# Attention score products of two heads side by side: queries and keys kept as pairs of heads on 128 rows

## The chip, the cores and the metric

The kernel runs on one core of a Trainium2 chip. A core has five engines with instruction queues of their own: TensorE (PE) multiplies matrices into PSUM, VectorE (DVE) and ScalarE (ACT) work element by element and read PSUM, GpSimd (POOL) works from SBUF, and SyncE (SP) issues DMAs. The metric is the device time of one execution in microseconds, the median of the runs.

## The reference

Two post-norm layers over 512 tokens of width 1024, in f32. Heads have 64 dimensions, so two heads fill the 128 partitions.

```
layer 0: proj = x @ w_in_swa                       # 12 query heads, 3 key/value heads, 4 memory queries
         q, k = partial_rope(q), partial_rope(k)   # the first 16 of 64 dimensions rotate
         self = softmax over {two chunks back and own chunk of 64 keys, sink} . v
         cross = softmax(qc . km * scale) . vm     # 4 heads, 256 memory tokens
         x = layer_norm(a*x + [self, cross] @ w_out); x = layer_norm(a*x + swiglu(x))
layer 1: proj = x @ w_in_fox                       # 12 query, key and value heads, 4 memory queries, 12 forget logits
         cum = cumsum(log_sigmoid(f_logit + b))
         self = softmax(q . k * scale + cum[query] - cum[key], causal) . v
         cross as above, out projection and norm as above
         x = layer_norm(a*x + moe(x))              # top 2 of 8 SwiGLU experts
```

## The kernel before

Every f32 operand is split into two f16 parts, high (f32 times a scale, rounded by an ACT copy, `high`) and low (what is left, by a DVE subtraction, `low`), and a product is three: high x high, high x low, low x high (`mm3`, L236). Weights arrive as chunks of 1 MB on SP's queue into three raw buffers; `Weights.tick` (L163) lets ACT write the high part of a piece (L149) and DVE the low one (L158). Seven split chunks are held (`NHL`). The order of all instructions is written out by hand (`manual_schedule`): each engine works through its own list in order.

The stages are: prologue and memory projections (0 to 54 us), sliding-window attention with memory heads (54 to 205), dense SwiGLU (205 to 580), forgetting layer (580 to 762 for its attention), out projection and routing (to 820), experts (to the end).

Attention goes in items. An item is one block of 128 queries against the keys that it sees: four memory heads (256 keys), four query heads of one key head (128 or 256 keys), or a pair of forgetting heads (128 to 512 keys). There are 8, 12 and 24 of them. `Att.step` (L589) runs items in a pipeline of four steps: scores (S, L488), maximum and exponentials (M), normalisation (N), transposes of the weights P (T, L545), low parts (L), output product (O, L562). ORDS and ORDX (L69) say in which order a step issues these, with a fill (F: a projection needed later) and weight ticks (W). In layer 0 the order is W F S O T M L N, in layer 1 w F S T M N L O. So in PE's list a fill comes ahead of the scores.

A fill of the forgetting layer is `qk_fill` (L1068): 24 products of 256 columns into a PSUM bank, then the evacuation of two heads' keys or queries. There are four such banks (L225), shared with the transposes and outputs.

How queries and keys are kept now:

- Queries have the high part of a head on 64 rows and its low part on the other 64 (`q_evac`, L398: two ACT copies, two DVE subtractions for a pair of heads). Keys have the high part of each head twice, on both halves (`k_evac`, L410: four ACT copies), and the low part once, two heads on 128 rows (two DVE subtractions). So one product over 128 rows gives (q high + q low) x k high (L497).
- The third product, q high x k low, works on 64 rows; for memory and forgetting heads those of two heads stand next to each other on different halves of the array (L506). Sliding-window keys are twice on 128 rows in both parts, and the product with the low part runs over 128 rows (L501).
- Masks and bias are added by products (L499): sliding window, an identity times a mask over all keys of the item; forgetting, a selector of 96 rows (three bf16 parts of the running sum for 12 heads) times the sums, and an identity times the causal mask.
- Rotary queries are turned by four transposes per token block, one per head, onto 64 rows (L823 to L826).

Of the kernel before, what the change touches and what calls it, by code (L numbers as in the profile page):

```python
# [209 lines left out]
def trunk_kernel(ctx, tc, x, mem, positions, w_in_swa, attn_sinks, w_in_fox, b_forget, w_mem_kv, w_out,  # L210
# [113 lines left out]
    identb = base.tile([128, 128], BF, name="identb")  # L324
    nc.vector.tensor_scalar(identb, jp, 0.0, None, op0=OP.is_equal)
# [72 lines left out]
    def q_evac(Q, i, n, src, sc, cols):  # L398

        todo = []  # L400
        for half in range(2):
            a, b = halves(half)
            idx = slice(i + half, i + half + 2 * n - 1, 2) if n > 1 else i + half
            todo.append((Q[a, idx, cols], Q[b, idx, cols], src(half)))
        for h, _, s in todo:
            high(h, s, sc)
        for h, l, s in todo:
            low(l, s, sc, h)

    def k_evac(KH, KL, heads, src, sc, cols):  # L410

        for half in range(2):
            for r in halves(half):
                high(KH[r, heads(half), cols], src(half), sc)
        for half in range(2):
            a = halves(half)[0]
            low(KL[a], src(half), sc, KH[a, heads(half), cols])

# [69 lines left out]
    def att_scores(it):  # L488
        nh, nk = it["nh"], it["nk"]
        b2 = bank2()  # L490
        it["S"] = b2.rearrange("p a n -> p (a n)").rearrange("p (h n) -> p h n", h=nh)[:, :, :nk]
        bank_of = lambda i: i * 2 // nh
        for i in range(nh):
            h = it["order"][i]
            o = it["S"][:, i, :]
            first = i == 0 or bank_of(i) != bank_of(i - 1)
# [3 lines left out]
            if it["rows"] is None:  # L500
                nc.tensor.matmul(o, it["q"](h), it["kl"](h), start=False, stop=True, skip_group_check=True)  # L501
        if it["rows"] is not None:
            for i in sorted(range(nh), key=lambda i: i % (nh // 2)):
                h = it["order"][i]
                a = it["rows"](h)
                nc.tensor.matmul(it["S"][:, i, :], it["q"](h)[a], it["kl"](h)[a], start=False, stop=True,  # L506
                                 skip_group_check=True)
# [108 lines left out]
    def mem_items(Qm, KM, VM, sp, blk0):  # L616
        for b in range(NT):
            bq = slice(b * 128, b * 128 + 128)
            yield dict(nh=MH, nk=ML, order=(0, 2, 1, 3), rows=lambda h: halves(h % 2)[0], pool=sp, sink=None, b=b,
                       blk=blk0, add=lambda h: [], q=lambda h, bq=bq: Qm[h // 2][:, h % 2, bq],  # L620
                       kh=lambda h: KM[0][:, h, :], kl=lambda h: KM[1][:, h // 2, :],
                       v=lambda h, kb: [v[:, kb, h * HD:h * HD + HD] for v in VM])

    def mem_kv(u, memT, KM, VM):
        def kpair(p):
# [3 lines left out]
            for k in range(KD):  # L629
                mm3(b, wh[:, k, c], wl[:, k, c], memT[0][:, k, :], memT[1][:, k, :], k == 0, k == KD - 1)  # L630
            k_evac(KM[0], KM[1][:, p, :], lambda hf: 2 * p + hf, lambda hf: b[64 * hf:64 * hf + 64, :], DS * SQ,
                   slice(0, ML))
# [14 lines left out]
    def qc_proj(wh, wl, c0, Qm):  # L647
        for p in range(MH // 2):
# [4 lines left out]
            q_evac(Qm[p], 0, 1, lambda hf: b[64 * hf:64 * hf + 64, :], DS * SQ, slice(0, S))  # L653
# [47 lines left out]
    def mem_tiles(pool):  # L701
        return ((pool.tile([128, MH, ML], FH, name="KMh"), pool.tile([128, MH // 2, ML], FH, name="KMl")),
# [15 lines left out]
    nc.gpsimd.dma_start(sinks, bass.AP(tensor=attn_sinks.tensor, offset=attn_sinks.offset, ap=[[0, 128], [1, NH]]))  # L718
    smask = sp.tile([128, 256], BF, name="smask")
    nc.vector.memset(smask, 0.0)  # L720
    nc.vector.memset(smask[0:64, 192:256], NEG)
    nc.vector.memset(smask[64:128, 0:64], NEG)
# [15 lines left out]
    KL = sp.tile([128, 3, S], FH, name="KL")  # L738
    V = (sp.tile([128, NT, 192], FH, name="Vh"), sp.tile([128, NT, 192], FH, name="Vl"))
    Qm = sp.tile([128, 4, S], FH, name="Q4", bufs=3)  # L740
    Qm = [Qm[:, 0:2], Qm[:, 2:4]]
# [16 lines left out]
    nc.vector.tensor_copy(posf, pos)  # L758
    for j in range(8):
        nc.vector.tensor_scalar(ang[:, :, j], posf, INV_FREQ[j], None, op0=OP.mult)  # L760
# [52 lines left out]
    def rope_evac(g, qk, t):  # L813
# [8 lines left out]
        else:  # L822
            for k in range(4):  # L823
                nc.tensor.transpose(b[:64, k, :], qk[:, k, :], identf)
            high(Qg[g][0:64, :, c], b[0:64])
            low(Qg[g][64:128, :, c], b[0:64], 1.0, Qg[g][0:64, :, c])  # L826

    def swa_items(g):
        for b in range(NT):
# [4 lines left out]
            yield dict(nh=4, nk=nk, order=range(4), rows=None, pool=sp, b=b, blk=2 * g,  # L834
                       sink=sinks[:, 4 * g:4 * g + 4], add=lambda h, nk=nk: [(0, nk, identb, smask[:, 256 - nk:])],
                       q=lambda h, bq=bq: Qg[g][:, h, bq],
                       kh=lambda h, kc=kc: KH[:, g, kc], kl=lambda h, kc=kc: KL[:, g, kc],
# [6 lines left out]
    def swa_fill(which):  # L844
# [6 lines left out]
        if t == 0 and g is not None:  # L851
            Qg[g] = sp.tile([128, 4, S], FH, name="Q4", bufs=3)
# [1012 lines left out]
```

## Time and profile before

| what | value |
|---|---|
| median of 3 runs | 1661.68 us (1661.27 to 1664.03) |
| profiled execution | 1663.01 us; its span 1661.2 us |
| TensorE busy, weight loads busy | 1596.2 us, 1281.7 us |
| VectorE, ScalarE, GpSimd busy | 1229.1 us, 975.3 us, 266.0 us |
| mean granted clock of TensorE | 0.989 of full speed |
| HBM | 355.08 MB read, 12.39 MB written |

The span runs from the first to the last instruction. The busy time of TensorE counts a product from its start to its modelled end, and products overlap, so what one costs in a stream is the distance to the next one's start. "Idle before" is the time for which an engine stood still ahead of an instruction, and the releaser is what ended that. DVE and ACT work through their lists in order, so an evacuation can stand behind work that has nothing to do with it.

### The profile page before, as it was taken

To read this page: it belongs to the slowest core of one execution; us is meant where nothing else is said; L and a number is where in the kernel's file an instruction comes from. 1 tells how busy PE (TensorE), PEld (TensorE's weight loads), DVE (VectorE), ACT (ScalarE), POOL (GpSimd) and SP (SyncE) were. 2 spreads that over 40 slices of the span, in tenths; PEclk is the share of its full clock that TensorE was granted. 3 is DMA by queue.
4 is the path that set the end of the run, shared out by engine and by line. 5 is a ranking of instruction groups with operands and counts; after the bars stand their busy time and mean duration, and the time that the engine had idled before them with its cause. 6 is when DMAs were issued, how large, how long until landed. Compare 5 with 4: busy or idle time off the path is not lost.

```text
span 1661.2 us, 42749 instructions
## 1 busy us (share of the span) xinstructions
PE 1596.2 (96%) x18452; PEld 1281.7 (77%) x18452; DVE 1229.1 (74%) x1826; ACT 975.3 (59%) x1499; POOL 266.0 (16%) x264
## 2 busy tenths in 40 slices
PE   7998999999999999999799999999999999999996
PEld 6785664444444747765699999999999999999994
DVE  6798643333534568786899698996979979699997
ACT  6776243333211457664477677776877778665773
POOL 0443100000200000003130140201303031130251
PEclk9999999999999999999899999999999999999998
DMA  7511033332631142111699899999999999999993
GB/s 266 178 52 52 3 127 125 102 102 90 213 120 54 52 129 75 52 52 39 224 353 335 301 387 387 371 349 304 389 362 371 364 315 376 336 289 370 349 369 126
DMA packets 180531, 370.13 MB, mean 223 GB/s; under 512 B 6573, under 2 KB 49581, under 8 KB 180336
## 3 DMA queue, kind: packets, MB, share of 16 engines
q1 hardware_dynamic: 173264, 343.48, 57.9%
q0 software_dynamic: 4768, 15.47, 4.0%
q10 hardware_dynamic: 2304, 8.39, 1.4%
q8 instruction: 146, 2.39, 0.6%
q14 instruction: 49, 0.40, 0.1%
HBM read 355.08 MB, written 12.39 MB: 221 GB/s over the span
## 4 chain that ended last, share of the span: by engine, by line
PE 43%; issue 3%; POOL 2%; ACT 1%; DVE 1%; DMA 1%; POOLq 0%; ACTq 0%; DVEq 0%
PE bk L1401 9%; PE bk L1403 9%; PE bk L1402 9%; PE bk L1432 4%; PE bk L1430 4%; PE bk L1431 4%; ACT wh L149 1%; POOL act L1419 1%; PE bk L239 1%; PE bk L237 1%; PE bk L238 1%; DVE wl L158 1%; POOL expert_sums L1334 1%; PE bk L1451 1%; PE bk L1342 1%
## 5 line engine op out<-in xcount | busy, mean ns | idle before, releaser
L158 DVE SCALAR_TENSOR_TENSOR wl<-raw,wh 128x1048 f16<-128x1048 f32 (+3 forms) x654 | 794.4, 1264 | 105.0 <-ACT wh L149 104.7
L149 ACT ACTIVATE wh<-raw 128x1048 f16<-128x1048 f32 (+3 forms) x654 | 640.9, 1041 | 100.2 <-PE bk L239 40.4
L1401 PE MATMUL bk<-xa,wh 128*128 128x160 f16 (+3 forms) x1280 | 261.2, 232 | 5.6 <-DMA lng<-in_ln_ffn_g_dram 5.6
L1402 PE MATMUL bk<-xa,wh 128*128 128x160 f16 (+3 forms) x1280 | 261.1, 232 | 0.0
L1403 PE MATMUL bk<-xa,wl 128*128 128x160 f16 (+3 forms) x1280 | 261.1, 232 | 0.0
L1401 PEld LDWEIGHTS <-wh 128*128 128x128 f16 x2560 | 250.9, 98 | 6.4 <-issue 5.7
L1402 PEld LDWEIGHTS <-wh 128*128 128x128 f16 x2560 | 250.9, 98 | 2.7 <-issue 2.4
L1403 PEld LDWEIGHTS <-wl 128*128 128x128 f16 x2560 | 251.0, 98 | 0.0
L1432 PE MATMUL bk<-act,wl 128*128 128x160 f16 (+6 forms) x1232 | 235.3, 227 | 1.2 <-DVE wl L158 1.2
L1430 PE MATMUL bk<-act,wh 128*128 128x160 f16 (+6 forms) x1232 | 235.3, 227 | 0.0
L1431 PE MATMUL bk<-act,wh 128*128 128x160 f16 (+6 forms) x1232 | 235.2, 227 | 0.0
L1401 PE MATMUL bk<-xe,wh 128*128 128x128 f16 (+2 forms) x1280 | 223.2, 221 | 2.2 <-DVE sa L1417 1.4
L1403 PE MATMUL bk<-xe,wl 128*128 128x128 f16 (+2 forms) x1280 | 223.1, 221 | 0.0
L1402 PE MATMUL bk<-xe,wh 128*128 128x128 f16 (+2 forms) x1280 | 223.1, 221 | 0.0
L237 PE MATMUL bk<-xTh,wh 128*128 128x512 f16 (+2 forms) x656 | 206.5, 325 | 7.7 <-DVE KLx L234 6.2
L239 PE MATMUL bk<-xTh,wl 128*128 128x512 f16 (+2 forms) x656 | 206.1, 324 | 2.8 <-DVE wl L158 2.8
L238 PE MATMUL bk<-xTl,wh 128*128 128x512 f16 (+2 forms) x656 | 206.2, 324 | 0.5 <-DVE xTl L234 0.5
L1419 POOL TENSOR_TENSOR act<-sa,act 128x512 f16<-128x512 f32 (+6 forms) x40 | 106.9, 2673 | 282.4 <-ACT act L231 282.4
L237 PEld LDWEIGHTS <-wh 128*128 128x128 f16 x944 | 93.1, 99 | 57.7 <-DVE KLx L234 7.2
L239 PEld LDWEIGHTS <-wl 128*128 128x128 f16 x944 | 93.2, 99 | 52.1 <-DVE wl L158 4.9
L238 PEld LDWEIGHTS <-wh 128*128 128x128 f16 x944 | 93.3, 99 | 47.5 <-issue 1.6
L1432 PEld LDWEIGHTS <-wl 128*128 128x128 f16 x1232 | 120.5, 98 | 1.6 <-DVE wl L158 1.6
(350 smaller groups left out, 2756.1 us busy)
## 6 DMA issues: line engine op xcount, KB each, us to landing
raw<-in_w_exp_in_dram SPq DMA_DIRECT2D x176, 1024.0 KB, 8.5
raw<-in_w_exp_out_dram SPq DMA_DIRECT2D x85, 1024.0 KB, 8.9
raw<-in_w_ffn_in_dram SPq DMA_DIRECT2D x22, 1024.0 KB, 5.4
raw<-in_w_out_dram SPq DMA_DIRECT2D x8, 1024.0 KB, 5.1
raw<-in_w_ffn_out_dram SPq DMA_DIRECT2D x8, 1024.0 KB, 5.6
raw<-in_w_in_fox_dram SPq DMA_DIRECT2D x8, 1024.0 KB, 5.3
raw<-in_w_mem_kv_dram SPq DMA_DIRECT2D x4, 1024.0 KB, 6.9
raw<-in_w_in_swa_dram SPq DMA_DIRECT2D x4, 896.0 KB, 8.9
```

Source lines behind the costliest of these rows:

```text
L149: self.nc.scalar.activation(h[:, p:e], t[:, p:e], AF.Copy, scale=SW)
L158: self.nc.vector.scalar_tensor_tensor(l, src, SW, h, op0=OP.mult, op1=OP.subtract)
L237: nc.tensor.matmul(o, lh, rh, start=first, stop=False, **kw)
L238: nc.tensor.matmul(o, lh, rl, start=False, stop=False, **kw)
L239: nc.tensor.matmul(o, ll, rh, start=False, stop=last, **kw)
L1401: nc.tensor.matmul(o, wh[:, k, c], xe[0][:, k, :C], start=first, stop=False, skip_group_check=True)
L1402: nc.tensor.matmul(o, wh[:, k, c], xe[1][:, k, :C], start=False, stop=False, skip_group_check=True)
L1403: nc.tensor.matmul(o, wl[:, k, c], xe[0][:, k, :C], start=False, stop=k == KD - 1, skip_group_check=True)
L1419: lambda: nc.gpsimd.tensor_sub(act[1][:, j, :C], sa[:, :, :C], act[0][:, j, :C])]
L1430: nc.tensor.matmul(o, wh[:, k, c], act[0][:, kk, :C], start=first, stop=False, skip_group_check=True)
L1431: nc.tensor.matmul(o, wh[:, k, c], act[1][:, kk, :C], start=False, stop=False, skip_group_check=True)
L1432: nc.tensor.matmul(o, wl[:, k, c], act[0][:, kk, :C], start=False, stop=kk == KF - 1, skip_group_check=True)
```

## The change

Queries and keys of two heads are kept as one tile of high parts and one of low parts, both on 128 rows (head A on rows 0 to 63, head B on 64 to 127). An evacuation is then one ACT copy and one DVE subtraction. All three score products of a head run on its 64 rows, and so do bias and mask. They are issued in turn for two heads of a pair, whose results go to two different PSUM banks:

```diff
-            nc.tensor.matmul(o, it["q"](h), it["kh"](h), start=first, stop=False, skip_group_check=True)
-            for lo, n, a, bb in it["add"](h):
-                nc.tensor.matmul(o[:, lo:lo + n], a, bb, start=False, stop=False, skip_group_check=True)
...
+        for pr in range(nh // 2):
+            both = [(half, it["S"][:, pr + half * nh // 2, :], it["parts"](2 * pr + half)) for half in range(2)]
+            n = len(both[0][2])
+            for j in range(n):
+                for half, o, parts in both:
+                    lo, m, r, a, c = parts[j]
+                    r = halves(r)[0]
+                    nc.tensor.matmul(o[:, lo:lo + m], a[r], c[r], start=pr == 0 and j == 0, stop=j == n - 1,
+                                     skip_group_check=True)
+    def products(h, nk, Q, K):
+        return [(0, nk, h % 2, Q[i], K[k]) for i, k in ((0, 0), (1, 0), (0, 1))]
```

Evacuations, in `mem_kv`, `qc_proj` and `qk_fill`:

```diff
-            if which:
-                k_evac(QK[p][1], QK[p][2][:, r], lambda hf: hf, src, DS * SQ, r)
-            else:
-                q_evac(QK[p][0], 0, 1, src, DS * SQ, r)
+            o = QK[p][which]
+            high(o[:, 0, r], b, DS * SQ)
+            low(o[:, 1, r], b, DS * SQ, o[:, 0, r])
```

Rotary queries (two transposes of two heads each), sliding-window mask (only the edges of 64 keys that need one) and forgetting bias and mask (64 rows):

```diff
-            for k in range(4):
-                nc.tensor.transpose(b[:64, k, :], qk[:, k, :], identf)
-            high(Qg[g][0:64, :, c], b[0:64])
-            low(Qg[g][64:128, :, c], b[0:64], 1.0, Qg[g][0:64, :, c])
+            for k in range(2):
+                nc.tensor.transpose(b[:, k, :], qk[:, 2 * k:2 * k + 2, :].rearrange("p i d -> p (i d)"), identf)
+            high(Qg[g][0][:, :, c], b[:, :2, :])
+            low(Qg[g][1][:, :, c], b[:, :2, :], 1.0, Qg[g][0][:, :, c])
...
+                edges = [(nk - 64, 64, h % 2, half_id[:, 0], smask)] + [(0, 64, h % 2, half_id[:, 1], smask)] * (nk > 128)
+                return products(h, nk, [q[:, h // 2, bq] for q in Qg[g]], [k[:, g, kc] for k in KHL]) + edges
...
+                return products(h, nk, [Q[:, i, bq] for i in range(2)], [K[:, i, :nk] for i in range(2)]) + \
+                    [(0, nk, h, sel[:, 2 * p + h, :], CB[:, :nk])] + \
+                    [(128 * b, 128, h, half_id[:, j], cmask[:, j]) for j in range(2)]
```

The set-up follows: `half_id` (a shifted identity for each half, four small DVE operations) replaces `identb`, `cmask` is made for each half, `smask` is 64 columns, the sinks are copied into the new order of heads, the selectors `sel` have 128 rows (two comparisons and four comparisons with an addition of 768 columns on DVE, where there were six comparisons), and the three bf16 parts of the running sum are put together with a factor per row (`share`), instead of copied to three groups of 32 rows:

```diff
-            nc.vector.tensor_copy(CB[32 * i:32 * i + 32, :], ch[32 * i:32 * i + 32, :])
+            if i == 0:
+                nc.vector.tensor_scalar(CB, ch, share[:, 0:1], None, op0=OP.mult)
+            else:
+                nc.vector.scalar_tensor_tensor(CB, ch, share[:, i:i + 1], CB, op0=OP.mult, op1=OP.add)
```

## Rows read from the trace of the kernel before

**Rows 1.** The page, part 1: busy time, share of the span, instructions of each engine.

```profile
PE 1596.2 (96%) x18452; PEld 1281.7 (77%) x18452; DVE 1229.1 (74%) x1826; ACT 975.3 (59%) x1499; POOL 266.0 (16%) x264
```

**Rows 2.** Busy time by stretch: length; PE, PEld, DVE, ACT, POOL; granted clock, DMA share, GB/s.

```profile
54.00:86.00 32.00, 30.38 (x330) 26.46 (x329) 24.72 (x37) 23.21 (x62) 18.17 (x58) 1.00 0.43 145
86.00:122.00 36.00, 34.21 (x400) 29.63 (x400) 34.30 (x75) 25.49 (x86) 15.76 (x45) 1.00 0.18 60
122.00:205.00 83.00, 78.70 (x674) 50.07 (x672) 62.65 (x142) 40.97 (x103) 21.72 (x35) 0.98 0.08 27
...
632.00:762.00 130.00, 120.85 (x1183) 87.28 (x1181) 106.97 (x246) 88.58 (x233) 4.81 (x5) 0.97 0.15 50
```

**Rows 3.** Waits of PE's weight loads, 592 to 762: us, times, longest us.

```profile
PEld L237 <- DVE KLx L234: 7.2, 5, 2.6
...
PEld L239 <- DVE wl L158: 3.3, 1, 3.3
```

**Rows 4.** Timeline of PE, a forgetting item: start us, us, engine, line, what.

```profile
686.63 0.39 PE L497 MATMUL bk<-KHx,Qx 128*128 128x512 f16 x1
686.85 0.38 PE L499 MATMUL bk<-CB,sel 96*128 96x512 bf16 x1
...
687.57 0.22 PE L499 MATMUL bk<-cmask,identb 128*128 128x128 bf16 x1
687.72 0.39 PE L506 MATMUL bk<-KLx,Qx 64*128 64x512 f16 x2
```

**Rows 5.** Timeline of PE, scores of a memory item (x4: four merged).

```profile
56.23 0.60 PE L497 MATMUL bk<-KMh,Q 128*128 128x256 f16 x4
56.76 0.39 PE L506 MATMUL bk<-KMl,Q 64*128 64x256 f16 x4
```

**Rows 6.** Timeline of PE, end of a sliding-window item's scores, then its output products.

```profile
118.73 0.27 PE L501 MATMUL bk<-KL,Q 128*128 128x256 f16 x1
118.94 0.25 PE L572 MATMUL bk<-PTh,Vh 128*64 128x128 f16 x2
119.02 0.22 PE L572 MATMUL bk<-PTl,Vh 128*64 128x128 f16 x2
119.07 0.22 PE L572 MATMUL bk<-PTh,Vl 128*64 128x128 f16 x2
```

**Rows 7.** Timeline of PE, the transposes of two rotary evacuations.

```profile
116.66 1.04 PE L824 MATMUL bk<-identf,qk 128*64 128x128 f32 x8
```

**Rows 8.** Timeline of ACT, a key evacuation.

```profile
694.24 1.54 ACT L231 ACTIVATE KHx<-bk 64x256 f16<-64x256 f32 x4
```

**Rows 9.** Timeline of DVE, the same key evacuation; last column: idle before, releaser.

```profile
695.82 0.86 DVE L234 SCALAR_TENSOR_TENSOR KLx<-bk,KHx 64x256 f16<-64x256 f32 x2 [0.99 <-ACT KHx L231]
```

**Rows 10.** Timeline of PE, the first product of two fills.

```profile
696.73 0.35 PE L237 MATMUL bk<-xTh,wh 128*128 128x256 f16 x1 [2.44 <-DVE KLx L234]
...
720.36 0.28 PE L237 MATMUL bk<-xTh,wh 128*128 128x256 f16 x1 [2.41 <-DVE KLx L234]
```

**Rows 11.** Groups of instructions by form, 54 to 205: count, busy us, mean ns, idle before.

```profile
L234 DVE SCALAR_TENSOR_TENSOR Q<-bk,Q 64x512 f16<-64x512 f32 x13 | 8.7, 683 | 2.2 <-ACT Q L231 1.9
...
L234 DVE SCALAR_TENSOR_TENSOR mixTl<-bk,mixTh 128x256 f16<-128x256 f32 x16 | 6.7, 421 | 6.2 <-ACT mixTh L231 6.0
```

**Rows 12.** Busy time by stretch, right behind the two fills (granted clock: third from the end).

```profile
696.00:700.00 4.00, 3.27 (x16) 2.38 (x17) 3.89 (x11) 2.58 (x8) 0.00 (x0) 0.60 0.81 264
720.00:724.00 4.00, 3.64 (x19) 2.62 (x20) 3.90 (x10) 2.21 (x8) 0.00 (x0) 0.59 0.69 249
```

**Rows 13.** Busy time by stretch, where constants and selectors are made.

```profile
428.00:448.00 20.00, 20.00 (x95) 9.04 (x94) 15.71 (x108) 5.59 (x7) 8.77 (x16) 1.00 0.73 232
```

**Rows 14.** Timeline of DVE, the bias rows' last copy and what follows.

```profile
605.08 0.28 DVE L1043 COPY CB<-ch 32x512 bf16<-32x512 bf16 x1
606.96 0.69 DVE L234 SCALAR_TENSOR_TENSOR Vxl<-bk,Vxh 128x512 f16<-128x512 f32 x1 [1.59 <-ACT Vxh L231]
```

**Rows 15.** Waits of PE, 800 to 835: us, times, longest us.

```profile
PE bk L1401 <- DMA lng<-in_ln_ffn_g_dram: 5.6, 1, 5.6
```

More of the change, by code (lines that the diff above doesn't have):

```diff
@@ L323, in trunk_kernel @@
     nc.vector.tensor_scalar(identf, jp, 0.0, None, op0=OP.is_equal)
-    identb = base.tile([128, 128], BF, name="identb")
-    nc.vector.tensor_scalar(identb, jp, 0.0, None, op0=OP.is_equal)
+    half_id = base.tile([128, 2, 128], BF, name="half_id")
+    for a in range(2):
+        for j in range(2):
+            r = slice(64 * a, 64 * a + 64)
+            nc.vector.tensor_scalar(half_id[r, j], jp[r], 64.0 * (j - a), None, op0=OP.is_equal)
     xtok = base.tile([128, NT, D], FT, name="xtok")
@@ L396, in halves, with pair_evac @@
         return slice(64 * half, 64 * half + 64), slice(64 - 64 * half, 128 - 64 * half)
[L398 to L417, printed above, removed]
+    def pair_evac(T, i, src, cols):
+        high(T[0][:, i, cols], src, DS * SQ)
+        low(T[1][:, i, cols], src, DS * SQ, T[0][:, i, cols])
     def ln_load(lnp, g, b, eng=nc.scalar, **kw):
@@ L618, in mem_items @@
             bq = slice(b * 128, b * 128 + 128)
-            yield dict(nh=MH, nk=ML, order=(0, 2, 1, 3), rows=lambda h: halves(h % 2)[0], pool=sp, sink=None, b=b,
-                       blk=blk0, add=lambda h: [], q=lambda h, bq=bq: Qm[h // 2][:, h % 2, bq],
-                       kh=lambda h: KM[0][:, h, :], kl=lambda h: KM[1][:, h // 2, :],
+            yield dict(nh=MH, nk=ML, order=(0, 2, 1, 3), pool=sp, sink=None, b=b, blk=blk0,
+                       parts=lambda h, bq=bq: products(h, ML, [q[:, h // 2, bq] for q in Qm], [k[:, h // 2, :] for k in KM]),
                        v=lambda h, kb: [v[:, kb, h * HD:h * HD + HD] for v in VM])
@@ L833, in swa_items, with parts @@
             kc = slice(k0 * 128, k0 * 128 + nk)
[L834 to L837, printed above, removed]
+            def parts(h, bq=bq, kc=kc, nk=nk):
+                edges = [(nk - 64, 64, h % 2, half_id[:, 0], smask)] + [(0, 64, h % 2, half_id[:, 1], smask)] * (nk > 128)
+                return products(h, nk, [q[:, h // 2, bq] for q in Qg[g]], [k[:, g, kc] for k in KHL]) + edges
+            yield dict(nh=4, nk=nk, order=(0, 2, 1, 3), parts=parts, pool=sp, b=b, blk=2 * g,
+                       sink=sinks[:, 4 * g:4 * g + 4],
                        v=lambda h, kb, k0=k0: [v[:, k0 + kb, g * HD:g * HD + HD] for v in V])
@@ L887, in trunk_kernel @@
     cx, cp = phase("masks")
-    cmask = cp.tile([128, 128], BF, name="cmask")
-    nc.vector.tensor_scalar(cmask, jp, 0.0, NEG, op0=OP.is_gt, op1=OP.mult)
+    cmask = cp.tile([128, 2, 128], BF, name="cmask")
+    for a in range(2):
+        for j in range(2):
+            r = slice(64 * a, 64 * a + 64)
+            nc.vector.tensor_scalar(cmask[r, j], jp[r], 64.0 * (j - a), NEG, op0=OP.is_gt, op1=OP.mult)
     upto = cp.tile([128, 256], FT, name="upto")
@@ L892, in trunk_kernel @@
     nc.vector.memset(upto[:, 128:], 1.0)
[L893 removed]
+    sel = cp.tile([128, NH, 128], BF, name="sel")
+    share = cp.tile([128, 3], FT, name="share")
     fx, fp = phase("ffn")
@@ L1021, in trunk_kernel @@
     nc.scalar.activation(fe, fe, AF.Ln, bias=1.0)
-    CB = op.tile([96, S], BF, name="CB")
-    lf = op.tile([128, NT, 96], FT, name="PTl", bufs=2)
+    CB = op.tile([128, S], BF, name="CB")
+    lf = op.tile([128, NT, 128], FT, name="PTl", bufs=2)
     nc.gpsimd.memset(lf, 0.0)
     def log_f():
-        for i in range(3):
-            nc.vector.scalar_tensor_tensor(lf[:, :, 32 * i:32 * i + NH], fl, 0.0, fe, op0=OP.min, op1=OP.subtract)
+        for a in range(2):
+            for i in range(3):
+                r = 64 * a + 6 * i
+                nc.vector.scalar_tensor_tensor(lf[:, :, r:r + 6], fl[:, :, a::2], 0.0, fe[:, :, a::2], op0=OP.min,
+                                               op1=OP.subtract)
     def cums():
-        b = bank()[:96, :]
+        b = bank()
         for i in range(NT):
@@ L1076, in f @@
             if p not in QK:
-                QK[p] = [op.tile([128, 2, S], FH, name=n, bufs=NQK) for n in ("Qx", "KHx")]
-                QK[p].append(op.tile([128, S], FH, name="KLx", bufs=NQK))
+                QK[p] = [op.tile([128, 2, S], FH, name=n, bufs=NQK) for n in ("Qx", "Kx")]
             b = bank()[:, :t1 - t0]
```

71 lines of the change are left out of this document (31 added, 40 removed).

## The prediction

> **What bounds the kernel now.** I read the page first: TensorE (PE) is busy 96% of the span [rows 1], so a change to PE's work pays only where PE is also what the others wait for. The change touches two stretches, so next I read the busy table for them: sliding-window attention from 54 to 205 us, and the forgetting layer's attention, whose own heads run from 632 to 762 us [rows 2]. In each stage PE is the fullest engine but one: from 86 to 122 us VectorE (DVE) is busy 34.3 of 36 us, beside PE's 34.2. There the two are tied, and PE alone cannot give time back. In the forgetting stage PE is busy 120.9 of 130 us, DVE 107.0.
>
> Then the list of waits of PE's weight loads, for 592 to 762 us [rows 3]: 7.2 us in five waits for the low half of a key block (KLx, written by DVE), and one of 3.3 us for a weight split. These are not product time. The projection that comes next needs a PSUM bank that the key evacuation still holds.
>
> **The change part by part.**
>
> *Score products, forgetting layer.* A block of nk keys and two heads takes now, per head, one 128-row product, one bias product and one mask product of 128 columns, and per pair of heads one pair of 64-row products. In time: 5 passes over nk and 2 over 128 columns. A 512-column pass takes 0.22 us (686.63 to 686.85) and the pair of 64-row products, both 512 wide, lasts 0.39 us from first start to last end, as one of 512 columns alone does: the two ran side by side [rows 4]. After: 3 passes for the pair's three score products, one for its two bias products, 2 of 128 columns for the mask: 4 nk + 256. One pass over nk goes. nk is 128, 256, 384 and 512, at 0.055, 0.11, 0.165 and 0.22 us: 0.55 us for one pair of heads, six pairs: 3.3 us.
>
> *Score products, sliding window.* Now 3 passes per head, 12 for four heads; a 256-column pass takes 0.11 us (four, each lasting 0.27, end 0.60 after the first one's start) [rows 5], and a pair on half the array 0.055 us for 128 columns (119.02 to 119.07) [rows 6]. A block of 256 keys costs 12 x 0.11 = 1.32 us. After: two pairs of heads, each 3 passes of 256 and two of 64 columns. A 64-column pair isn't in the trace. Below, it is half of the 128-column one, 0.03 us; above, the whole of it, 0.055; I take 0.04, nearer the columns than the whole. So 2 x (0.33 + 0.08) = 0.82 us: 0.50 less (0.44 to 0.54), nine times: 4.5 us. The blocks of 128 keys go from 12 x 0.055 = 0.66 to 2 x (0.165 + 0.04) = 0.41, three times: 0.75 us. Together 5.2 us (4.6 to 5.7).
>
> *Switch of the array.* From full rows to another shape PE loses time: 118.73 to 118.94 is 0.21 us where the step is 0.11, and 687.57 to 687.72 is 0.15 where it is 0.055 [rows 4, 6]. So 0.10 us. Memory and forgetting items have a switch to 64 rows now, in the middle of their scores; after, it comes ahead of them. Sliding-window items have none today and get one, since their scores stand between a full-row fill and the half-column output product, which already pays its own: 12 x 0.10 = 1.2 us more.
>
> *Memory items.* Four 128-row passes and two pairs now, six pairs after: six passes either way, no change. Here two pairs stand one behind the other: four products last 0.39 us, each 0.27, so the second pair started 0.12 us after the first, against 0.11 for full rows [rows 5].
>
> *Rotary queries.* Each of 12 evacuations loses two of its four transposes. Eight end 1.04 us after the first one's start; if the last takes 0.27 us as other products do, seven steps fill 0.77, 0.11 each [rows 7]: 24 x 0.11 = 2.6 us. PE's sum is 3.3 + 5.2 + 2.6 - 1.2 = 9.9 us.
>
> *Key and query evacuations.* A 256-column key block is four copies on ScalarE (ACT), 1.54 us, and two on DVE, 0.86 us [rows 8, 9]; PE's projection meanwhile waits 2.44 us (last column of the row at 696.73), and as long once more at 720.36 [rows 10]. After, it is one copy and one subtraction of the same columns. Rows don't set their time: 128x256 takes 421 ns on DVE [rows 11], 64x256 430 [rows 9]. So 2.40 us becomes 0.38 + 0.43 = 0.8 and each wait shrinks by up to 1.6. The two of 2.6 us give 1.6 each, the three others, which sum to 2.0 (7.2 - 2 x 2.6), nearly all: 5.2 us. The wait for the weight split stands behind a query evacuation of 512 columns on the same DVE queue; half of its DVE and ACT work goes, and I take 1.3 of its 3.3 us. Together 6.5 us; between 3 (what is late next is the exponential, or DVE's normalisation of the weights P, for which the transposes wait already) and 9 (every such wait goes).
>
> *The clock.* Behind such a wait the granted clock falls: to 0.60 on average in 696 to 700 us and 0.59 in 720 to 724 [rows 12], which is a stretch at 1.2 GHz instead of 2.4, some 40% of 4 us, 1.6 us each. A shorter wait should not bring it down. I take both: 3.2 us, between 0 and 3.2.
>
> *Given back.* In 86 to 122 us PE's share of the above is 3.1 us: six steps of 0.45 less the switch of 0.10 each, and some five rotary evacuations of 0.22. DVE has 1.7 us of slack there [rows 2] and loses 0.26 us at each query evacuation (683 to 421 ns, half the columns) [rows 11], six of them: 1.6 us. Part of the slack is waits that stay; I take back 1.4 us. In the forgetting stage the gains come to 3.3 + 6.5 + 3.2 = 13 us; DVE falls from 107.0 by some 20 evacuations of 0.43 (five or six pairs of heads, two halves, keys and queries, each one DVE operation less), to 98 of 117 us, no emptier than now. A fifth of 13, 2.5 us, I take back as new waits for DVE.
>
> *At no cost.* Half-identity, mask and selector set-up: more small DVE work, the most between 428 and 448 us, where PE is busy 20.0 of 20 us on weights split ahead [rows 13]; uncovered, it would be 1 to 2 us. The bias rows: DVE's three 0.28 us copies become longer by some 0.4 us each, and DVE is then idle 1.59 us before its next operation [rows 14]; uncovered, 1.2 us. The small sink copy needs a transfer issued at the start. The memory keys of layer 0 are evacuated in the prologue, which I take as paced by its transfers; if not, two evacuations give 1.6 us each. No DMA issue is moved.
>
> *Sum:* 9.9 + 6.5 + 3.2 - 1.4 - 2.5 = 15.7 us. The profiled execution took 1663.0 us (span 1661.2, 1.8 around it), so 1647.3; the median of the runs shown is 1.3 lower, so 1646 us. The dense layers between and the experts behind see the same work, shifted. The experts begin with PE waiting 5.6 us for a transfer [rows 15]; its issue follows the attention's end, so I take it as shifted too.
>
> **The rivals.**
>
> *DVE keeps the pace* (14%). The PE time is saved and turns into waits. For: the tie in 86 to 122 us, and DVE's large share elsewhere [rows 2]. Against: the evacuations take work off DVE and ACT as well. Then the shorter products give only half of 9.9, the evacuation waits the low end, the clock nothing: 5 + 3 = 8 us: 1654.
>
> *Weight loads come into the open* (6%): slower. Today 64-row products run at most two pairs in a row; after, four to six, and each half of the array gets its next weights while it still multiplies. There are 48 memory, 114 sliding-window and 144 forgetting pairs, 306, of which 40 exist. If each new one pays what a switch pays, where nothing is hidden, that is 266 x 0.10 = 27 us: 1673. It turns slower than before from 0.06 us a pair. Against: the second pair in [rows 5] paid 0.01. This is what the Trainium skill says in "TensorE: Matmul & The Clock Gate", Part 3, "The mechanism": a weight load overlaps running products only when it goes to another row group. By that rule a pair's own next loads would be exposed; full-row products stepping at 0.11 us, each with its own load, disagree with it in this trace [rows 5].
>
> *The freed time is absorbed* (5%). If the transfer at the experts' start [rows 15] were paced from elsewhere, 5.6 us of the gain would end there, and with DVE keeping the pace little is left: about 1660.
>
> *More than summed* (9%). All evacuation waits go (9), nothing is given back, and the waits for P shrink by 2 us: 9.9 + 9 + 3.2 + 2 = 24 us: 1638.
>
> **How the numbers follow.** The forecast has 66% with its own range from 1641 to 1651 us. Faster by over 0.2% (3.3 us, about what a measurement of this kernel tells from no change) is the forecast, the first and the last rival: 0.89; same 0.05; slower 0.06. The range reaches to the ends of the likely cases, 1638 to 1656.
>
> **What would show it.** In the trace after: scores as pairs of 64 rows started within some ns of each other, pairs 0.11 us apart for 256 columns; a gap of 0.10 us ahead of sliding-window scores; one ACT copy and one DVE subtraction per key block; no wait near 2.6 us for a key block and no fall of the clock at those places; 54 to 205 us shorter by some 6 us, 592 to 762 by some 10. It is wrong if pairs step at much more than their columns, if waits for P or for the weight split grow by what the key waits lose, or if the experts' stage lengthens.

## The result, and the profile after

The changed kernel takes 1643.98 us (median of 4 runs, 1643.21 to 1644.89) against 1662.24 of the kernel before beside it (4 runs): ratio 0.9887, 95% interval 0.9875 to 0.9899. The prediction was 1646, between 1638 and 1656. The profiled execution took 1643.21 us, with a span of 1641.4.

The page, part 1, of the changed kernel (answers to [rows 1]):

```profile
PE 1580.5 (96%) x18640; PEld 1269.8 (77%) x18640; DVE 1211.7 (74%) x1807; ACT 947.6 (58%) x1439; POOL 263.4 (16%) x265
```

PE's share is what it was; 15.7 us of its busy time went, and DVE and ACT lost 17 and 28 us. Where the time went is read by stage. The table follows four places in PE's and DVE's timelines: from the first memory score to the last maximum of the sliding-window layer; from the first maximum of the forgetting layer to the first router product (attention, out projection, routing); from there to the first expert product; from there to the last instruction (us, between the starts of these instructions). The kernels in the lower part are those of the experiments.

| kernel | sliding window | forgetting | to the experts | experts |
|---|---|---|---|---|
| before | 102.5 | 179.3 | 45.9 | 841.5 |
| changed | 97.9 | 161.0 | 46.0 | 845.4 |
| split evacuations | 98.0 | 180.3 | 50.2 | 841.4 |
| one head after the other | 97.9 | 166.1 | 45.4 | 846.3 |
| one pair more | 98.1 | 163.3 | 46.2 | 842.7 |
| code shifted by 48 | 97.9 | 161.0 | 45.4 | 842.7 |
| before, shifted by 136 | 102.5 | 179.2 | 45.7 | 841.3 |
| more on GpSimd, shifted by 48 | 97.4 | 160.7 | 46.0 | 841.5 |
| work behind the evacuation | 100.0 | 164.3 | 45.3 | 846.4 |
| twice on VectorE | 103.3 | 161.0 | 45.4 | 846.2 |
| before, shifted by 112 | 103.2 | 181.0 | 46.2 | 844.6 |
| evacuation first, shifted by 48 | 97.8 | 161.0 | 45.5 | 842.5 |

So the sliding window gave 4.6 us, the forgetting layer 18.3, and the experts took 3.9 back. What is left of the difference in span (19.8) is 0.8: the first score comes 0.95 earlier, and 0.2 is lost in the stretches between. The kernels that share that prologue reach the first score anywhere from 54.5 to 56.1 us, so this is not put down to the change.

The busy table of the changed kernel by stretch, the same stages as in [rows 2] (length; PE, PEld, DVE, ACT, POOL; granted clock, DMA share, GB/s):

```profile
53.00:85.00 32.00, 30.02 (x350) 26.13 (x348) 22.52 (x37) 22.82 (x62) 17.57 (x60) 1.00 0.39 126
85.00:119.00 34.00, 31.55 (x432) 26.55 (x431) 32.38 (x77) 23.61 (x84) 15.30 (x42) 1.00 0.20 64
119.00:200.00 81.00, 75.83 (x710) 47.53 (x708) 61.10 (x142) 40.55 (x103) 21.75 (x35) 0.98 0.08 27
...
623.00:750.00 127.00, 123.84 (x1350) 88.48 (x1349) 105.23 (x242) 79.17 (x205) 9.02 (x8) 1.00 0.16 51
```

From 85 to 119 us, where the two were tied, DVE alone is the fullest engine now: 32.4 of 34 us against 31.6. In the forgetting stage PE fills 97.5% (123.84 of 127), and the granted clock is 1.00 where it was 0.97 [rows 2].

Waits of PE in the forgetting layer, before (592.7 to 774 us) and after (587 to 750): us, times, longest us.

```profile
PE bk L237 <- DVE KLx L234: 6.2, 3, 2.4
PE bk L239 <- DVE wl L158: 2.8, 1, 2.8
PE bk L556 <- DVE P L543: 2.1, 5, 0.6
PE bk L572 <- DVE KLx L234: 1.4, 1, 1.4
```

```profile
PE bk L239 <- DVE wl L158: 1.4, 1, 1.4
PE bk L541 <- DVE PTl L234: 1.1, 1, 1.1
PE bk L237 <- DVE Kx L234: 0.9, 1, 0.9
PE bk L541 <- DVE P L528: 0.8, 1, 0.8
```

The waits for a key tile went from 7.6 us in four to 0.9 in one, that for a weight split was halved, and those for the normalised weights P shrank as well.

Timeline of PE after, a sliding-window item ([rows 6]); a memory item ([rows 5]); a forgetting item of 512 keys, to be laid beside [rows 4]:

```profile
93.86 0.38 PE L809 MATMUL bk<-identf,qk 128*128 128x128 f32 x2
94.17 0.39 PE L487 MATMUL bk<-KH,Q 64*128 64x256 f16 x4
94.40 0.27 PE L487 MATMUL bk<-KL,Q 64*128 64x256 f16 x2
94.51 0.22 PE L487 MATMUL bk<-smask,half_id 64*128 64x64 bf16 x4
94.57 0.38 PE L487 MATMUL bk<-KH,Q 64*128 64x256 f16 x4
...
587.14 0.28 PE L487 MATMUL bk<-KMh,Qx 64*128 64x256 f16 x2
587.26 0.27 PE L487 MATMUL bk<-KMh,Kx 64*128 64x256 f16 x2
...
654.08 0.82 PE L487 MATMUL bk<-Kx,Qx 64*128 64x512 f16 x6
654.74 0.38 PE L487 MATMUL bk<-CB,sel 64*128 64x512 bf16 x2
654.96 0.28 PE L487 MATMUL bk<-cmask,half_id 64*128 64x128 bf16 x4
```

x2 with one start is a pair of heads side by side: 587.14 to 587.26 is 0.12 us for two products of 256 columns. Four pairs of 512 columns take 0.88 us (654.08 to 654.96), 0.22 each. In the sliding-window item a pair of heads takes 0.40 us (94.17 to 94.57), for which 0.41 was taken; of it, two pairs of 64 columns take 0.06. The two transposes ahead start 0.31 us before the scores, where two steps fill 0.22: the switch of the array, 0.1 us, as priced.

Timelines of ACT, DVE and PE after: the one key evacuation for which PE still waits ([rows 8 to 10]):

```profile
679.74 0.39 ACT L231 ACTIVATE Kx<-bk 128x256 f16<-128x256 f32 x1
680.23 0.42 DVE L234 SCALAR_TENSOR_TENSOR Kx<-bk,Kx 128x256 f16<-128x256 f32 x1
680.70 0.27 PE L237 MATMUL bk<-xTh,wh 128*128 128x256 f16 x1 [0.92 <-DVE Kx L234]
```

1.54 and 0.86 us became 0.39 and 0.42, and the wait of 2.44 is 0.92.

Timeline of PE after, where the experts begin:

```profile
795.99 0.32 PE L1407 MATMUL bk<-xa,wh 128*128 128x160 f16 x1 [5.90 <-DMA lng<-in_ln_ffn_g_dram]
796.10 0.34 PE L1408 MATMUL bk<-xa,wh 128*128 128x160 f16 x1
796.23 0.34 PE L1409 MATMUL bk<-xa,wl 128*128 128x160 f16 x1
799.87 0.29 PE L1407 MATMUL bk<-xa,wh 128*128 128x160 f16 x1 [3.29 <-issue]
```

The wait ahead of the first product is 5.9 us, where [rows 15] has 5.6. What is new stands three products later: PE stops for 3.64 us, and the releaser is "issue": nothing that another engine did. The stage lost 3.9 us. The granted clock is at its lower level until 803.6 us, 7.6 us into the stage; in the kernel before it rises after 3.4.

### The profile page after: what moved, and what is told of

The parts are those of the page before. It is cut to its first block, busy times and chain, and to the rows that moved or that the text cites. A ratio compares the mean times of both kernels' runs of the same rounds, so it can differ in the third digit from the quotient of the medians.

```text
span 1641.4 us, 43009 instructions
## 1 busy us (share of the span) xinstructions
PE 1580.5 (96%) x18640; PEld 1269.8 (77%) x18640; DVE 1211.7 (74%) x1807; ACT 947.6 (58%) x1439; POOL 263.4 (16%) x265
## 3 DMA queue, kind: packets, MB, share of 16 engines
q8 instruction: 148, 2.42, 0.6%
## 4 chain that ended last, share of the span: by engine, by line
PE 40%; issue 3%; DVE 3%; DMA 2%; ACT 2%; POOL 2%; ACTq 0%; POOLq 0%; DVEq 0%
PE bk L1407 8%; PE bk L1409 8%; PE bk L1408 8%; PE bk L1438 4%; PE bk L1436 4%; PE bk L1437 4%; DVE wl L158 2%; DMA raw<-in_w_exp_in_dram 1%; ACT wh L149 1%; POOL act L1425 1%; PE bk L239 1%; PE bk L237 1%; PE bk L238 1%; POOL expert_sums L1340 1%; PE bk L1457 1%
## 5 line engine op out<-in xcount | busy, mean ns | idle before, releaser
L1425 POOL TENSOR_TENSOR act<-sa,act 128x512 f16<-128x512 f32 (+6 forms) x40 | 103.4, 2586 | 284.8 <-ACT act L231 284.8
```

The lines of the kernel that those rows point to most:

```text
L1425: lambda: nc.gpsimd.tensor_sub(act[1][:, j, :C], sa[:, :, :C], act[0][:, j, :C])]
```

## The experiments

### What the evacuations were worth

Split evacuations: the forgetting layer's alone, with their old count of instructions.

```
-            high(o[:, 0, r], b, DS * SQ)
-            low(o[:, 1, r], b, DS * SQ, o[:, 0, r])
+            for half in range(2):
+                a = halves(half)[0]
+                for _ in range(2 if which else 1):
+                    high(o[a, 0, r], b[a], DS * SQ)
+            for half in range(2):
+                a = halves(half)[0]
+                low(o[a, 1, r], b[a], DS * SQ, o[a, 0, r])
```

> The changed kernel with the old count of evacuation instructions in the forgetting layer alone: a key block is four copies of 64 rows on ScalarE (two of them write what another has written) and two subtractions on VectorE, a query block two and two; the products stay in pairs. Theory: of the 18.2 us by which the forgetting layer's attention became shorter, 3.3 are columns and the rest, some 11 to 14, was the evacuations holding PE's bank, with the fall of the clock behind it. Then 10 to 14 us come back in the stretch that begins with the first score of that layer, the waits of PE's projections for the key tile are over 2 us again, and the time is near 1655. Rival: the paired products did it, because their scores end sooner and everything behind them starts sooner. Then under 3 us come back and the time stays under 1647.

Measured: 1661.81 us, ratio 0.9991 (0.9982 to 1.0000). The forgetting stage is 180.3 us: all of the gain is gone, 19.3 us, more than the 10 to 14 that the theory asked for. Timelines of ACT, DVE and PE at a key evacuation:

```profile
689.48 1.58 ACT L231 ACTIVATE Kx<-bk 64x256 f16<-64x256 f32 x4
691.10 0.86 DVE L234 SCALAR_TENSOR_TENSOR Kx<-bk,Kx 64x256 f16<-64x256 f32 x2 [1.03 <-ACT Kx L231]
692.01 0.28 PE L237 MATMUL bk<-xTh,wh 128*128 128x256 f16 x1 [2.48 <-DVE Kx L234]
```

The busy table over the 4 us that follow this wait and the other long one:

```profile
692.00:696.00 4.00, 3.99 (x22) 2.95 (x23) 3.81 (x9) 1.90 (x6) 0.00 (x0) 0.57 0.61 228
716.00:720.00 4.00, 4.00 (x24) 2.74 (x24) 3.40 (x8) 1.90 (x6) 0.00 (x0) 0.57 0.51 198
```

Both long waits are back, each with its fall of the clock (0.57; [rows 12]), and the waits for P are 4.1 us. A third fall, from 614.0 to 617.4 us, is new: at half the clock it costs up to 1.7 us (an estimate), which the kernel before did not pay. So with the old evacuations the saved columns buy nothing here: they become waits.

Work behind the evacuation: the new evacuation, and behind it the instructions that the old one had more.

```
+            idle = op.tile([128, 2, S], FH, name="idle", bufs=1)
+            a = halves(0)[0]
+            for _ in range(3 if which else 1):
+                high(idle[a, 0, r], o[a, 0, r])
+            low(idle[a, 1, r], o[a, 0, r], 1.0, o[a, 1, r])
```

> The changed kernel with the instructions that the old evacuations had more in the forgetting layer put behind the new ones, on a scratch buffer: three copies of 64 rows on ScalarE and one subtraction on VectorE for a key block, one and one for a query block. The engines have about the old load, but the bank of PE's projection comes free after one copy and one subtraction. The split evacuations cost 18.7 us there. Theory: what costs is the bank held while PE's next projection wants it; then under 5 us come back, and the time stays under 1649. Rival: what costs is the load on VectorE and ScalarE, which the maxima, exponentials and normalisations behind it wait for; then 10 us or more come back, 1655 or over.

Measured: 1646.84 us, ratio 0.9893 (0.9878 to 0.9908). Groups of instructions on the scratch tile, with smallest, median and largest time in ns:

```profile
L231 ACT ACTIVATE idle<-Kx x33: 416/417/631, 616.8 to 711.7; 64x256 f16<-64x256 f16 x30, 64x512 f16<-64x512 f16 x3
L234 DVE SCALAR_TENSOR_TENSOR idle<-Kx x11: 417/417/683, 617.6 to 711.7; 64x256 f16<-64x256 f16 x10, 64x512 f16<-64x512 f16 x1
```

With the query's there are 44 such copies and 22 subtractions, some 28 us of engine time at 0.42 each. They cost the forgetting stage 3.3 us (164.3 against 161.0). The same number of instructions ahead of the release of the bank costs 19.3. So of the 19.3 the load itself accounts for some 3.3, and the rest is the bank that the next projection waits for. (The sliding window of this run has the changed kernel's code and is 2.1 us longer; its clock fell there for 6.8 us, see the last section.)

### What the columns are worth

One pair more: a pair of products of zero weights in each pair of heads.

```
+    none = base.tile([128, 128], FH, name="none")
+    nc.vector.memset(none, 0.0)
...
-                return products(h, nk, [q[:, h // 2, bq] for q in Qg[g]], [k[:, g, kc] for k in KHL]) + edges
+                return products(h, nk, [q[:, h // 2, bq] for q in Qg[g]], [k[:, g, kc] for k in KHL]) + \
+                    [(0, nk, h % 2, none, KHL[0][:, g, kc])] + edges
...
+                    [(0, nk, h, none, K[:, 0, :nk])] + \
```

> The changed kernel with one pair of products more in each pair of heads, of zero weights against all keys of the block, in the sliding-window and in the forgetting items. By columns this costs PE 9 x 2 x 0.11 + 3 x 2 x 0.055 = 2.3 us in the sliding-window stage and 0.55 us for each of six pairs of heads, 3.3 us, in the forgetting stage. Theory: PE now sets the forgetting stage, which becomes longer by 3.0 to 3.5 us; in the sliding-window stage VectorE shares the pace, so under 1.5 us of the 2.3 show there, and the waits for VectorE shrink by the rest. In all 4 to 5 us, 1648.5. Rival one: PE sets both, 5.6 us. Rival two: VectorE now sets both, under 2 us.

Measured: 1643.08 us, ratio 0.9870 (0.9855 to 0.9885): no slower than the changed kernel, since the added instructions also moved the experts' code, and the stop there is gone (experts 842.7). By stage: 3.3 us of products make the forgetting stage 2.35 us longer, where 3.0 to 3.5 were expected, and 2.3 us of products make the sliding window 0.2 us longer. PE sets the one, not the other.

Twice on VectorE: the subtraction of the rotary query evacuations done twice.

```
-            low(Qg[g][1][:, :, c], b[:, :2, :], 1.0, Qg[g][0][:, :, c])
+            for _ in range(2):
+                low(Qg[g][1][:, :, c], b[:, :2, :], 1.0, Qg[g][0][:, :, c])
```

> The changed kernel with the subtraction of each of the 12 rotary query evacuations of the sliding-window layer done twice, to the same place: VectorE gets 12 operations of 0.41 us, 4.9 us, and PE nothing. One pair of products more for each pair of heads, 2.3 us on PE, made this stage only 0.2 us longer. Theory: VectorE sets the pace there, above all from 85 to 119 us, where six or seven of the evacuations lie; the way from the first memory score to the last maximum, 97.9 us, becomes 2 to 4 us longer. Rival: neither engine alone sets it, but the chain from step to step does, with room on both; then under 1 us.

Measured: 1647.25 us, ratio 0.9898 (0.9883 to 0.9913). The sliding window is 5.4 us longer, over the 2 to 4 expected. Part of it is the clock: the busy table of this kernel and of the changed one for the same 4 us.

```profile
135.00:139.00 4.00, 2.98 (x9) 1.59 (x10) 3.83 (x11) 1.97 (x6) 0.00 (x0) 0.50 0.00 0
```

```profile
135.00:139.00 4.00, 4.00 (x20) 1.67 (x17) 3.84 (x10) 3.52 (x11) 1.31 (x2) 1.00 0.00 0
```

One granted clock is 1.2 GHz, the other 2.4. PE's wait for a query's bank ahead of this had grown from 1.7 to 2.2 us; that it brought the clock down is not shown, since the same wait is 2.2 us in the run with more on GpSimd, and no fall follows there. The run with work behind the evacuation had a fall of the same length here (6.8 us) and no such work, and lost 2.1 us; by that some 3.3 of the 5.4 are the subtractions, within the 2 to 4. So work on DVE lengthens this stage, and work on PE hardly does (0.2 us for 2.3).

More on GpSimd: items of four heads normalise one head on DVE and three on GpSimd; the code is shifted by 48 too.

```
-            if h >= PN:
+            if h >= (1 if it["nh"] == 4 else PN):
```

> The changed kernel with the experts' code 48 instructions later, as in the experiment with 24 products more, and in items of four heads three heads' weights P normalised on GpSimd instead of two. This takes a 0.66 us operation of 256 keys off VectorE for each sliding-window item. Theory: VectorE sets the pace from 85 to 119 us, so the way from the first memory score to the last maximum of the sliding-window items becomes 1 to 3 us shorter than 97.9, and the time some 2 below that of the shift alone: 1637. Rival: P comes later from GpSimd, which is slower for one head and has the rotary work too, and the transposes wait for it; then the way is as long or longer.

Measured: 1639.13 us, ratio 0.9860 (0.9841 to 0.9879), as the shift alone. The sliding window is 0.5 us shorter (97.4), not 1 to 3. DVE got 1.6 us of air from 85 to 119 us, and 5.6 in the whole stage (busy 77.0 us, where it was 82.6), but the wait for the query's bank grew to 2.2 us, and transposes waited 0.7 for GpSimd. The rival was nearer: taking load off DVE does not by itself bring this stage forward.

Evacuation first: steps without a projection issue the evacuations that are left ahead of the weight splits; shifted by 48 too.

```
+        att.order = ORDS if p else "FWSOTMLN"
```

> The changed kernel with the experts' code 48 instructions later, and with one more move: in the sliding-window steps that have no projection, the evacuations of rotary queries that are left are issued ahead of the two weight splits instead of behind them. In the changed kernel PE waits 1.98 us at 131.36 for a bank that such an evacuation holds; ScalarE does two splits, 2.01 us, from 130.45 first. Theory: that wait goes, the way from the first memory score to the last maximum (97.9 us) becomes 1.5 to 2 us shorter, and the fall of the clock in that stage may go with it; the time is 2 us under that of the shift alone, 1636 to 1637. Rival: the splits are then late themselves and the projection that follows waits for its weights, or VectorE stays the bound; then the way is no shorter.

Measured: 1638.52 us, ratio 0.9846 (0.9833 to 0.9860); the sliding window is 97.8 us. Waits of PE from 119 to 155 us, changed kernel and this one:

```profile
PE bk L541 <- DVE Q L234: 1.7, 1, 1.7
PE bk L809 <- POOL qk L795: 0.7, 1, 0.7
```

```profile
PE bk L237 <- DVE xtok L417: 1.2, 1, 1.2
PE bk L809 <- POOL qk L795: 0.8, 1, 0.8
```

The wait of 1.7 us went, and one of 1.2 came 8 us later, for a residual sum that DVE does: the second rival. Several chains through DVE are close behind each other in this stage.

### Whether the heads must alternate

One head after the other: the same products, all of one head first.

```
-            for j in range(n):
-                for half, o, parts in both:
+            for half, o, parts in both:
+                for j in range(n):
```

> The changed kernel with the same score products in another order: all of one head, then all of the other, instead of the two heads in turn. Theory: two products on different halves of the rows run beside each other only where they stand next to each other, so the passes double: 4 x 1280 + 4 x 256 columns for each of six pairs of heads of the forgetting layer, at 0.11 us for 256 columns 15.8 us; in the sliding-window layer 9 x 0.82 + 3 x 0.41 = 8.6; in the 8 memory items 0.66 each, 5.3. Together up to 30 us, 1674, slower than the kernel before by 11. Rival: PE looks ahead far enough to bring both halves together, or the pairs are not what gave the time; then the time stays within 3 us of 1644.

Measured: 1648.97 us, ratio 0.9912 (0.9898 to 0.9925). Theory and rival both miss: the forgetting stage is 5.1 us longer, not 15.8, and sliding window and memory items do not change. Timeline of PE, a memory item and an item of 512 keys:

```profile
585.15 0.29 PE L487 MATMUL bk<-KMh,Qx 64*128 64x256 f16 x2
585.27 0.28 PE L487 MATMUL bk<-KMh,Kx 64*128 64x256 f16 x2
...
653.96 0.84 PE L487 MATMUL bk<-Kx,Qx 64*128 64x512 f16 x4
654.61 0.38 PE L487 MATMUL bk<-CB,sel 64*128 64x512 bf16 x1
654.63 0.38 PE L487 MATMUL bk<-Kx,Qx 64*128 64x512 f16 x1
```

In the memory item three products of one head are issued, then three of the other; the fourth starts with the first, at 585.15 (x2). PE has taken it ahead of the second and third, which share the first one's half of the rows. With six products a head (the rows from 653.96 us) the other head's begin 0.45 us late and end late, and only that overhang is lost.

### What stopped the experts

Code shifted by 48: products that never run, in the loop that PE branches over.

```
+        for i in range(24):
+            nc.tensor.matmul(b[:, 16:18], oh[:, i % NT, :128], tid[:, i % NT, :], start=i == 0, stop=i == 24 - 1)
```

> The changed kernel with 24 products more in the body of the loop over overflowing experts, which runs no time with this input: nothing more is computed, but PE's code behind the loop stands 48 instructions later. Theory: PE stops for 3.6 us after some 12 products of the first expert (796.23 to 799.87) because its code comes in blocks of 256 instructions, 16 KB, and the place to which it branches over the loop is near the end of such a block; 48 instructions on, the place is near the start of the next block, PE has some 100 products to run while the one behind it comes, and 3.5 to 4.5 us go (the clock rises sooner too): 1640. Rival: the stop comes from weights or tables that are late; then it stays where it is, and the time at 1644.

Measured: 1638.90 us, ratio 0.9852 (0.9838 to 0.9865). Timeline of PE at the first expert:

```profile
795.82 0.31 PE L1407 MATMUL bk<-xa,wh 128*128 128x160 f16 x1 [5.65 <-DMA lng<-in_ln_ffn_g_dram]
795.93 0.34 PE L1408 MATMUL bk<-xa,wh 128*128 128x160 f16 x1
796.06 0.34 PE L1409 MATMUL bk<-xa,wl 128*128 128x160 f16 x1
796.20 0.34 PE L1407 MATMUL bk<-xa,wh 128*128 128x160 f16 x1
```

No stop: the fourth product follows after 0.14 us. With experts at 842.7, 2.7 us of the 3.9 are back in these profiles, and the median is 5.1 us lower. Of the 1.2 that are missing the clock may be 1.0 (an estimate): it rises 5.3 us into the stage here, 3.4 in the kernel before, and 1.9 us more at half speed cost half of that. The trace's DMA packets show what PE stopped for. In the changed kernel a packet of 16 KB in queue 8, whose kind is "instruction", moves from 797.06 to 798.41 us, within the stop, and PE goes on 1.46 us after its end. Here such a packet moves from 796.96 to 798.05, and PE works through it. (The stop comes behind 3 products, not behind the dozen that the expectation says.)

Before, shifted by 136: the same loop of products in the kernel before.

```
+        for i in range(68):
```

> The kernel before, with 68 products more in the body of the loop that runs no time: PE's code behind the loop stands 136 instructions later, and its first instruction then has the same place within a block of 256 as in the changed kernel. Theory: the stop of some 3.5 us after the first dozen of the experts' products comes from that place alone; it appears here too, at about 820 us, and the time is 3 to 5 us over the kernel before, 1667. Rival: it belongs to the earlier end of the attention in the changed kernel; then there is no stop and no difference.

Measured: 1663.78 us, ratio 0.9996 (0.9987 to 1.0005), and no stop. The count was wrong by 24, as the next expectation says.

Before, shifted by 112:

```
+        for i in range(56):
```

> The kernel before again with products added to the body of the loop that runs no time, 56 now, so that the code behind the loop stands 112 instructions later. The shift by 136 was counted from the program before its fp32 products get their weight loads; these count too, and the kernel before has 24 more of them ahead of the loop than the changed one. With them the place at which the changed kernel's stop begins is 112 on. Theory: what decides is the place of the branch's target in its block of 256 instructions. After it PE stopped behind 3 products where the target stood at 0, behind 2 where it stood 2 instructions later, before the first where it stood 6 later, and not at all at 48 or 192 later. So the kernel before stops here behind 3 products, at about 820 us, for 3 to 4 us, and the time is 3 to 4.5 us over the kernel before, 1667. Rival: the stop hangs on the changed kernel's other timing; then none appears here, as at 136.

Measured: 1667.53 us, ratio 1.0023 (1.0014 to 1.0033), with the stop where it was to be:

```profile
820.51 0.34 PE L1403 MATMUL bk<-xa,wl 128*128 128x160 f16 x1
824.15 0.29 PE L1401 MATMUL bk<-xa,wh 128*128 128x160 f16 x1 [3.29 <-issue]
```

PE's packet of 16 KB moves from 821.85 to 822.80 us, again within the stop. PE's recorded instructions ahead of the first expert product number 12057 in the changed kernel and 11689 in the kernel before, 368 apart, so 112 more put the target 256 from where the changed kernel has it. In instructions from where the changed kernel's target lies: 0 (changed, one head after the other, work behind the evacuation, before + 112) stops behind 3 products, each of which is a weight load and a product; 2 (twice on VectorE) stops behind 2; 6 (split evacuations) has no product ahead of the stop, and its first one comes after a wait of 10.1 us instead of 5.9; 24, 48 and 192 have no stop, nor has the kernel before. So the theory holds in both kernels.

## Why the prediction was right, and where it was not

The total was 2 us off, and that is in part luck, since errors of both signs are in it: the forgetting layer gave 18.3 us where 10.5 were forecast, the sliding window 4.6 where 5.2 were, and the experts took 3.9 that the sum did not have. With the code shifted, the same change measures 1638.90 us, which is close to the price of the rival "more than summed" (1638, 9%).

*Columns, forgetting layer* (3.3 us): right. The starts of PE's products give 3.4 us less of columns there, at 2.4 GHz. *Sliding window and rotary transposes* (5.2 and 2.6), *switch of the array* (+1.2): together 6.6 less for PE, whose busy time in the table's stretch fell by 6.0 (96.4 to 90.4 us). The switch is 0.1 where it was read (93.86 to 94.17), as priced; in the forgetting layer switches shrank by some 0.7 us, which was not predicted.

*Key and query evacuations* (6.5 us, between 3 and 9): mis-sized. The waits for a key tile lost 6.7 us (7.6 to 0.9), where 5.2 were taken, and the wait for the weight split 1.4, where 1.3 were: 8.1. The working let each wait shrink by the evacuation's own 1.6 us, and left a rest of 1.0 in both long ones; one is 0.9 now, the other is gone. The waits for P fell from 2.1 to 0.8, which was counted under the rival "more than summed". By the starts of PE's products, gaps too short for the list included, some 16 us of waits in this layer became some 5.

*The clock* (3.2): right. Both dips are gone, two stretches of 3.4 us at 1.2 GHz, whose products take 3.4 us less.

*Given back*: in the sliding window 1.4 was taken back, and PE's idle time grew by 1.4 (6.1 to 7.5 us); the stage gave 4.6 where 5.2 + 2.6 - 1.2 - 1.4 = 5.2 stood. That DVE has a hold on this stage was read rightly [rows 2]: the pair that was added and the doubled subtraction show it. What the saved products alone gave there is not shown. DVE's busy time fell by 5.5 us in the same stretch (88.1 to 82.6), and 2.3 us of products put back cost only 0.2, so a part of the 4.6 is likely due to the lighter evacuations. In the forgetting stage 2.5 was taken back and nothing was: DVE is at 83% there (105.2 of 127), and nothing waits for it long. That step failed: a high busy share is not a tie. With it and the evacuations, 3.3 + 6.5 + 3.2 - 2.5 = 10.5 us were forecast for this stage, which gave 18.3.

*Experts, shifted*: failed. The wait in [rows 15] did shift, but PE's code behind the loop moved too, and cost 3.9 us. No row of before shows that price, and the count of PE's instructions was no term of the sum. A longer experts' stage is one of the signs by which the prediction called itself wrong.

*At no cost*: the bias rows' last operation took 0.75 us instead of 0.28, and DVE still idled 0.67 us behind it; from the last sliding-window maximum to the first of the forgetting layer it is 435.8 us in both kernels.

*Rivals.* Weight loads did not come into the open: pairs step by their columns, whole trains of them. By that the rule of "TensorE: Matmul & The Clock Gate", Part 3, "The mechanism" in the Trainium skill (a load overlaps only with another row group's products) is contradicted for the pairs too; the other case that the section names, a load into the background weight buffer, would fit these rows. The freed time was not absorbed: the experts begin 23.7 us earlier, behind a like wait. DVE sets the pace in the sliding window alone, and not by itself there, and "more than summed" is what the forgetting layer did.

Open: what the short evacuations would give without the paired products. Keys laid out in pairs need the products in pairs, so this was not tried. The saved pass by itself bought nothing with the split evacuations; with the short ones, the same pass put back cost 2.35 us.

## What to carry to other kernels

Price an evacuation by what waits for its bank, not by its engine time: the same instructions cost 3.3 us behind the release of the bank and 19.3 ahead of it. Where one stage holds two engines at the same fill, a saving on one is worth little until the chain through the other is shortened too. A change that alters the number of PE's instructions ahead of a branch can win or lose some 4 us that have nothing to do with what it was made for; shift the code before believing a difference of that size. The best version run here is the changed kernel with the code shifted, 0.985 of the kernel before, with or without the evacuations first.

## What the runs showed of the hardware

- A branch over a loop costs more where its target lies close to the end of a block of code: 3.6 us of stop, or 4.2 us on the wait ahead, and then the clock at its lower level for longer. The block is 256 instructions: targets 256 apart gave the same stop in the two kernels, and the profile of the changed kernel counts 148 packets and 2.42 MB in queue 8, 16 KB each, for PE's 37280 products and loads, 252 a packet. In both kernels PE goes on 1.4 us after such a packet has arrived (798.41 to 799.87, and 822.80 to 824.15). The Trainium skill ("Runtime: NRT & Kernel Launch", "Instruction fetch mechanics") says that code comes in such blocks and that a taken branch makes the engine wait for the target's; the runs agree, and the stop after three products is a second wait, for the block behind the target's.
- PE starts products out of the order in which they are issued when they use the other half of its rows: in the memory items of the kernel with one head after the other the fourth starts with the first, ahead of two that were issued before it. The Trainium skill ("TensorE: Matmul & The Clock Gate", Part 2, "Step-by-step: what each phase is for") says that products keep their order and weight loads alone are taken ahead; this trace disagrees.
- The same wait of 1.7 us for a query's bank was followed by 6.8 us at 1.2 GHz in the run with work behind the evacuation and by none in the changed kernel, whose sliding-window code is the same (it fell there at 158 us, for 3.4). With three heads on GpSimd the wait is 2.2 us, and the clock does not fall in this stage at all. In the forgetting layer the wait of 2.8 us for a weight split is followed by a fall with split evacuations (614.0 us) and by none in the kernel before. So what decides the clock after such a wait is something that these rows don't show, and single stages differ by 2 us between like kernels.
